# A decoder trunk in which the output projection becomes two Strassen products around the pointwise projection

## Chip, cores and metric

The kernel runs on one core of a Trainium2 chip. The metric is device microseconds (us) of one execution; a run's time is that of the whole program. TensorE is PE in the profile (PEld is its weight load), VectorE is DVE, ScalarE is ACT, GpSimd is POOL, and SyncE, which issues the kernel's DMAs, is SP.

## The reference

The kernel computes one layer for 1024 tokens and a model width of 1024:

```python
u = rms_norm(x, ln_g)
c_val, c_glu, c_gate, hq, hf, hi, hg = split(u @ w_in)       # seven parts of 1024 columns
y_conv = conformer(c_val, c_glu) @ w_pw2 + b_pw2             # pointwise projection
y_conv = y_conv * silu(c_gate)                               # the conv gate
y_hgrn = hgrn2(hq, hf, hi) * silu(hg)                        # eight heads of 128
h = x + concat([y_conv, y_hgrn]) @ w_out                     # w_out: 2048 x 1024
gate = sigmoid(rms_norm(h, pe_norm_g) @ w_pg)
h = h + gate * (p @ w_pp)
out = rms_norm(h, final_g)
```

All is float32. Every matrix product on PE is made of two float32r parts of each factor, a high part and the rest, as high x high + high x low + low x high: three matmuls for one.

## The kernel before

Tokens are cut into eight blocks of 128, and for moving operands into two halves of 512; channels into eight blocks of 128. A split of an operand (`split`) is a copy on ACT into the high part and a subtraction on DVE into the low part. `prep` loads a weight block into a tile `raw` of the pool `wp`, which has three buffers of it, and splits it.

**The z stage** takes u (in SBUF, split, channels on partitions) through w_in, one block of 128 columns at a time: `ztile` preps the block and `product` makes two PSUM banks with 48 matmuls. The loop over the eight heads and channel groups does the conv and the heads; it leaves the conv's result in DRAM (`yc_d`) and each head's in `yh_d` (the tile sgT, whose last step are two multiplications on DVE, L443, that read the banks ot of PE's transposes). Last come the eight conv gates (`conv_gate`, column blocks 16 to 23, tiles wz16 to wz23): ACT takes the SiLU into sgc, and SP writes it to `sg_d`.

**The pointwise projection** loads yc into the pool `yp`, split (tiles ych, ycl). For each of eight column blocks m it preps wpw, loads the gate (sgr), makes two banks, and DVE adds the bias and multiplies with the gate (L570). The result is split at once into mch, mcl and stays in SBUF.

**The output projection** then takes 16 row blocks of w_out (eight for the pointwise result, eight for the heads, whose tiles yhr are loaded and split here into mhh, mhl) for the first four token blocks, with eight banks open: one per token block and column half. `residual` adds each bank to the residual h, a tile of x loaded into SBUF well ahead (L580, L595). A second pass does the other four token blocks, by column halves, with w_out loaded and split again. `norm_T` transposes the residual, scales and splits it. The gate's projection and the final norm are the tail.

Each engine takes its instructions in an order fixed when the program is built. A scheduler sets it: it takes the code in the order in which it is written, except where a `high_priority` number moves a step, as it does for the loads and splits of ztile's weights (2000 ahead) and for the late steps of heads and convs. A pool's tile with a tag is a ring of `bufs` buffers: a load into it waits until the last reader of the tile before it is done, and whatever stands behind that load on SP waits too.

Of the kernel before, what the change touches and what calls it, by code (L numbers as in the profile page):

```python
# [28 lines left out]
LATER_STATS, LATER_CONV, LATER_HEAD = 50, 330, 240  # L29
# columns of the transposed parameter table  # L30
# [5 lines left out]
def trunk_kernel(ctx: ExitStack, tc: tile.TileContext, x, p, ln_g, w_in, conv_w, conv_b,  # L36
# [12 lines left out]
    wp = ctx.enter_context(tc.tile_pool(name="wp", bufs=3))  # L49
    up = ctx.enter_context(tc.tile_pool(name="up", bufs=32))  # L50
# [10 lines left out]
    yh_d = [dpl.tile([P, T], F32, name=f"yh_d{m}") for m in range(G)]  # L61

    # ---------------------------------------------------------------- constants
# [7 lines left out]
    # per-channel parameters, channels on partitions  # L71
# [4 lines left out]
    def load_params(work):  # L76
# [11 lines left out]
        # lower bound: first row of the softmax over the layers  # L88
# [27 lines left out]
    def prep(src, shape, name):  # L116
        """A weight block: loaded, and split exactly into two float32r parts."""
# [13 lines left out]
    # ---------------------------------------------------------------- z phase  # L131
    uh = [[None] * G, [None] * G]
    ul = [[None] * G, [None] * G]
    with tc.tile_pool(name="st", bufs=1) as st:
        # layer embedding, projected: kept in DRAM until the gate is known
# [30 lines left out]
        def norm_x(hf, xs):  # L166
            """Normalised input of four token blocks, channels on partitions, split."""
# [14 lines left out]
        # masks[l][s, col]: where the key s is one that the score column couples to, the columns  # L182
        # being those of the block of 32 that s lies in
# [3 lines left out]
        def block_mask(dst, first, step_n, step_j, l):  # L187
            """Sets dst[s, n, j, i] where s is in the l keys from first + n step_n + j step_j."""
# [10 lines left out]
        def own_block(name, mf):  # L199
            """The columns of each row's own block out of those of the four blocks of 32."""  # L200
# [335 lines left out]
    for m in range(G):  # L536
        conv_gate(m)
# [16 lines left out]
    def load_split(src, hi, lo, k, name):  # L554
        raw = wp.tile([P, T], F32, tag="raw", name=name)
        nc.sync.dma_start(raw, src)
        for hf in range(2):
            split(hi[hf][k], lo[hf][k], halves(raw)[hf])

    ych, ycl = half_tiles(yp, "y", "yc")  # L560
    for k in range(G):
        load_split(yc_d[k], ych, ycl, k, f"ycr{k}")
# [167 lines left out]
```

## Time and profile before

| | us |
|---|---|
| median of three runs | 1146.96 |
| lowest, highest | 1146.39, 1148.70 |
| span of the profiled execution | 1146.5 |
| PE busy in it | 1124.8 |
| DVE, ACT, POOL busy in it | 739.5, 443.0, 72.0 |

The profiled execution is one run of the program; its span is 0.46 us under the median of the timed runs, and all rows below are from it. The last conv gates (blocks 20 to 23) run from 737.2 to 781.7 us, the pointwise projection from 781.7 to 868.7, the first half of the output projection from 868.7 to 955.7, the second half with the transposes around it from 955.7 to about 1050, and the gate's projection to the end. The page cuts the span into 40 slices of 28.7 us; a digit is the busy share of an engine in tenths. An engine's idle time counts only where what it holds up is on the way to the end.

### The profile page before, as it was taken

Reading aid. Unit: us, or ns where it says so; the run is one execution under the profiler, and the core shown is the slowest. Engines: PE = TensorE matmul, PEld = TensorE weight load, DVE = VectorE, ACT = ScalarE, POOL = GpSimd, SP = SyncE. Lnnn points to the kernel's source line nnn. Section 1 sums busy time; section 2 is a strip of 40 time slices with the busy share of each in tenths; the row PEclk is TensorE's granted clock in tenths of the full one; section 3 lists DMA queues with packets and bytes.
Section 4 is the critical chain, followed back from the end, with each engine's and each line's share of the span. In section 5 each row is a group of like instructions: output and inputs, shape, how many; then the busy total and the mean of one; then the engine's idle time right before and its main releaser. Section 6 shows DMA issues by size and latency. Waiting matters only on the chain.

```text
span 1146.5 us, 17744 instructions
## 1 busy us (share of the span) xinstructions
PE 1124.8 (98%) x7408; PEld 945.6 (82%) x7408; DVE 739.5 (65%) x1145; ACT 443.0 (39%) x811; POOL 72.0 (6%) x107
## 2 busy tenths in 40 slices
PE   6999999999999999999999999999999999999997
PEld 4888978889888789788898788888888888887886
DVE  3659579998499996599993896242334325226444
ACT  4823244253354442344532632442123324126333
POOL 3100001001001010010010010000000001001000
PEclk9899999999999999999999999999999999999999
DMA  7611121211111112111111112277335632334221
GB/s 247 236 37 55 37 66 30 74 55 39 55 57 56 59 35 74 56 37 56 57 56 56 57 56 93 74 242 254 110 92 165 195 99 77 107 109 149 92 92 56
DMA packets 85715, 104.60 MB, mean 91 GB/s; under 512 B 3290, under 2 KB 65754, under 8 KB 85634
## 3 DMA queue, kind: packets, MB, share of 16 engines
q1 hardware_dynamic: 85634, 103.46, 28.1%
q8 instruction: 58, 0.95, 0.3%
q14 instruction: 23, 0.19, 0.1%
HBM read 82.48 MB, written 20.97 MB: 90 GB/s over the span
## 4 chain that ended last, share of the span: by engine, by line
PE 89%; DVE 6%; DMA 2%; ACT 1%; issue 1%; SPq 0%; POOL 0%; POOLq 0%; ACTq 0%
PE z L241 14%; PE z L242 14%; PE z L243 14%; DVE y L452 4%; PE v L264 3%; PE v L265 3%; PE v L263 3%; PE pg L683 3%; PE pg L684 3%; PE pg L682 3%; PE oA L591 3%; PE pw L243 3%; PE pw L241 3%; PE oA L589 3%; PE oA L588 3%; PE pw L242 3%
## 5 line engine op out<-in xcount | busy, mean ns | idle before, releaser
L452 DVE SCALAR_TENSOR_TENSOR y<-vpad,par,y 128x1024 f32<-128x1024 f32 x232 | 288.8, 1278 | 1.1
L682 PE MATMUL pg<-gh,hh 128*128 128x512 f32 (+1 forms) x136 | 51.4, 378 | 0.0
L683 PE MATMUL pg<-gl,hh 128*128 128x512 f32 (+1 forms) x136 | 51.4, 378 | 0.0
L684 PE MATMUL pg<-gh,hl 128*128 128x512 f32 (+1 forms) x136 | 51.3, 377 | 0.0
L519 DVE TENSOR_TENSOR vpad<-z,gl 128x512 f32<-128x512 f32 x16 | 11.0, 691 | 42.7 <-PE z L243 42.7
L263 PE MATMUL v<-wv_0h,uh 128*128 128x256 f32 x128 | 36.7, 287 | 0.0
L265 PE MATMUL v<-wv_0h,ul 128*128 128x256 f32 x128 | 36.5, 285 | 0.0
L264 PE MATMUL v<-wv_0l,uh 128*128 128x256 f32 x128 | 36.5, 285 | 0.0
L263 PE MATMUL v<-wv_1h,uh 128*128 128x256 f32 x128 | 36.2, 283 | 0.0
L264 PE MATMUL v<-wv_1l,uh 128*128 128x256 f32 x128 | 36.2, 283 | 0.0
L265 PE MATMUL v<-wv_1h,ul 128*128 128x256 f32 x128 | 36.2, 283 | 0.0
L266 ACT ACTIVATE vt<-v 128x256 f32<-128x256 f32 x32 | 12.2, 382 | 58.9 <-PE v L265 58.9
L688 DVE TENSOR_TENSOR gt<-gt,pet 128x512 f32<-128x512 f32 (+1 forms) x17 | 11.2, 661 | 36.1 <-ACT gt L687 36.1
L108 POOL TENSOR_SCALAR ro<-sso 128x8 f32<-128x8 f32 x8 | 8.4, 1054 | 389.9 <-ACT on L129 389.9
L475 DVE TENSOR_SCALAR y<-yt,mv,ry 128x128 f32<-128x128 f32 x64 | 23.5, 404 | 13.1 <-POOL ry L109 13.1
L570 DVE SCALAR_TENSOR_TENSOR sgr<-pw,par,sgr 128x512 f32<-128x512 f32 x16 | 12.0, 750 | 30.1 <-PE pw L243 30.1
L437 ACT ACTIVATE on<-o,ro 128x128 f32<-128x128 f32 x64 | 18.5, 386 | 29.0 <-POOL ro L109 29.0
L682 PEld LDWEIGHTS pg<-gh,hh 128*128 128x128 f32 x136 | 25.6, 188 | 4.7
L683 PEld LDWEIGHTS pg<-gl,hh 128*128 128x128 f32 x136 | 25.6, 188 | 4.7
L684 PEld LDWEIGHTS pg<-gh,hl 128*128 128x128 f32 x136 | 25.6, 188 | 4.5
L483 ACT ACTIVATE yc<-yn,par 128x512 f32<-128x512 f32 x16 | 12.5, 778 | 39.8 <-PE yn L482 39.8
L129 ACT ACTIVATE on<-o 128x128 f32<-128x128 f32 x64 | 16.9, 278 | 23.3 <-PE up L409 18.9
(802 smaller groups left out, 3463.6 us busy)
## 6 DMA issues: line engine op xcount, KB each, us to landing
wz<-in_w_in_dram SPq DMA_DIRECT2D x48, 512.0 KB
wo<-in_w_out_dram SPq DMA_DIRECT2D x32, 512.0 KB
xt<-in_x_dram SPq DMA_DIRECT2D x8, 512.0 KB
pe_d<-pes SPq DMA_DIRECT2D x8, 512.0 KB
wv<-in_w_in_dram SPq DMA_DIRECT2D x8, 512.0 KB
yc_d<-yc SPq DMA_DIRECT2D x8, 512.0 KB
yh_d<-sgT SPq DMA_DIRECT2D x8, 512.0 KB
sg_d<-sgc SPq DMA_DIRECT2D x8, 512.0 KB
```

Source lines behind the costliest of these rows:

```text
L241: mm(z, lhsT=wh[:, k, :], rhs=mh[hf][k], start=k == 0, stop=False)
L242: mm(z, lhsT=wh[:, k, :], rhs=ml[hf][k], start=False, stop=False)
L243: mm(z, lhsT=wl[:, k, :], rhs=mh[hf][k], start=False, stop=k == G - 1)
L263: mm(z, lhsT=uh[hf][k][:, c], rhs=wh, start=k == 0, stop=False)
L264: mm(z, lhsT=uh[hf][k][:, c], rhs=wl, start=False, stop=False)
L265: mm(z, lhsT=ul[hf][k][:, c], rhs=wh, start=False, stop=k == G - 1)
L452: nc.vector.scalar_tensor_tensor(y[j % 2], vp[:, j:j + T], pcol(g, j), y[j % 2], op0=ALU.mult, op1=ALU.add)
L588: mm(z, lhsT=mixh[hf][k][:, c], rhs=wh[j], start=first, stop=False)
L589: mm(z, lhsT=mixh[hf][k][:, c], rhs=wl[j], start=False, stop=False)
L682: mm(z, lhsT=hh[k][:, c], rhs=gh[j][k][:, o:o + w], start=k == 0, stop=False)
L683: mm(z, lhsT=hh[k][:, c], rhs=gl_[j][k][:, o:o + w], start=False, stop=False)
L684: mm(z, lhsT=hl[k][:, c], rhs=gh[j][k][:, o:o + w], start=False, stop=k == G - 1)
```

## The change

The output projection is taken apart by halves of w_out. The heads' half is multiplied first, behind the conv gates; then comes the pointwise projection; then the half of the pointwise result, called the mixture. Each half is a product of 1024 tokens x 1024 channels x 1024 columns, done for one pair of token blocks after the other as a Strassen product (in Winograd's form): a pair's tokens, the channels' halves and the columns' halves make a 2 x 2 scheme, which takes seven products of 128 tokens x 512 channels x 512 columns instead of eight.

- `combos` loads the eight row blocks of a half of w_out (two at a time, each into a `raw`) and makes from them the seven weight combinations a, t1, t2, d, t3, c, t4, each in high and low part, 56 tiles in the new pool `cb`. For the heads' half it stands in the code between the fourth and the fifth conv gate and takes its `raw` from `wp`, whose ring wz20 shares; for the mixture's half it stands behind the first column block of the pointwise projection.
- `tokens` loads a pair's two channel halves (tiles mx) from DRAM, makes four sums on DVE and splits seven factors. `project` makes the seven products in three banks (za, zd, zb) that are never cleared in between; `put` adds or subtracts a bank into the two residual tiles as soon as a term of the sum is in it.
- The heads' residual tiles hx are loaded from x, one buffer for each block of a pair, and written to `h_d` behind the pair. Behind the pointwise projection they are loaded back into eight tiles h.
- The pointwise result goes to DRAM (`mc_d`) and its loads are those of `tokens`. The weights wpw now come as two halves from the pool `rg`, in tiles `s` that the yc loads and the sums share (four buffers).
- The gate's weights and the transposed residual take over tiles of `cb`; `norm_T` for both halves stands behind all pairs.
- The scratch for dynamic DMAs is set to 2048 bytes.

```diff
@@ the output projection's weights, and where they stand @@
-    for m in range(G):
+    def combos(row0, pool, bufs):
+        hi = {n: [] for n in XN}
+        lo = {n: [] for n in XN}
+        def part(n, k, src, sign=1.0):
...
+            nc.scalar.activation(h, src, AF.Copy, scale=sign)
+            nc.vector.scalar_tensor_tensor(lo[n][k], src, sign, h.bitcast(F32),
+                                           op0=ALU.mult, op1=ALU.subtract)
+        for k in range(KH):
+            rows = []
+            for i in range(2):
+                r = pool.tile([P, D], F32, tag="raw", bufs=bufs, name=f"wo{row0}_{k}_{i}")
+                o = row0 + (i * KH + k) * P
+                nc.sync.dma_start(r, w_out[o:o + P, :])
+                rows += halves(r)
+            a, b, c, d = rows
+            for n, t in (("a", a), ("c", c), ("d", d)):
+                part(n, k, t)
+            nc.vector.tensor_tensor(a, a, b, op=ALU.subtract)
+            part("t1", k, a)
+            nc.vector.tensor_tensor(a, a, d, op=ALU.add)
+            part("t2", k, a, -1.0)
+            nc.vector.tensor_tensor(b, d, b, op=ALU.subtract)
+            part("t3", k, b)
+            nc.vector.tensor_tensor(c, a, c, op=ALU.subtract)
+            part("t4", k, c)
+        return hi, lo
+    for m in range(G // 2):
         conv_gate(m)
+    xh, xl = combos(D, wp, 3)
+    for m in range(G // 2, G):
+        conv_gate(m)
@@ a pair of token blocks @@
+    def tokens(src, tb):
+        r0, r1 = (raw(src[i * H:(i + 1) * H, tb * P:(tb + 2) * P]
+                      .rearrange("(k p) t -> p k t", p=P), f"mx{src.name}{tb}_{i}")
+                  for i in range(2))
...
+    def project(src, tb, hA, hB):
+        f1, f5, f6, f3, f7, f2, f4 = tokens(src, tb)
+        za, zd, zb = (bank("z", f"o{n}{src.name}{tb}") for n in "adb")
...
+        mul(za, f1, "a", True, False)
+        put(hA, 0, za, ALU.add)
+        mul(zd, f5, "t1", True, False)
+        put(hB, 1, zd, ALU.subtract)
+        mul(za, f6, "t2", False, False)
+        put(hA, 1, za, ALU.add)
+        mul(zd, f3, "d", False, True)
+        put(hA, 1, zd, ALU.add)
+        mul(za, f7, "t3", False, False)
+        put(hB, 1, za, ALU.subtract)
+        mul(zb, f2, "c", True, True)
+        put(hA, 0, zb, ALU.add)
+        mul(za, f4, "t4", False, True)
+        put(hB, 0, za, ALU.subtract)
@@ the heads' half, ahead of the pointwise projection @@
+    with tc.tile_pool(name="hx", bufs=1, reuse_waits="tile") as hx:
+        for tb in range(0, G, 2):
+            hAB = []
+            for i in range(2):
+                t = hx.tile([P, D], F32, tag=f"h{i}", name=f"hx{tb + i}")
+                nc.sync.dma_start(t, x[(tb + i) * P:(tb + i + 1) * P, :])
+                hAB.append(t)
+            project(yh_d, tb, *hAB)
+            for i in range(2):
+                nc.sync.dma_start(h_d[tb + i], hAB[i])
@@ the pointwise projection @@
+            if m == 1:
+                xh, xl = combos(0, rg, 2)
...
+            nc.sync.dma_start(mc_d[m * P:(m + 1) * P, :], sg)
@@ the mixture's half @@
+    hs = [hp.tile([P, D], F32, name=f"h{tb}") for tb in range(G)]
+    for tb in range(G):
+        nc.sync.dma_start(hs[tb], h_d[tb])
...
-    hhA, hlA = norm_T(0)
...
+    for tb in range(0, G, 2):
+        project(mc_d, tb, hs[tb], hs[tb + 1])
```

**DVE between gate blocks 19 and 20.** Before, DVE does the last head's state (S) and its two last steps sgT (banks ot), with the low parts of wz22 and wz23 around them; wz20l and wz21l are further up:

```order
L414 SCALAR_TENSOR_TENSOR S_6583<-S_6583,F_128_6580,up_0_6596 128x128 x3
L414 SCALAR_TENSOR_TENSOR S_6583<-S_6583,F_128_6580,up_1_6605 128x128 x3
L114 TENSOR_TENSOR wz22l<-wz_7024,wz22h 128x1024
L443 SCALAR_TENSOR_TENSOR sgT_6019<-ot_0_6646,par,sgT_6019 128x512
L114 TENSOR_TENSOR wz23l<-wz_7084,wz23h 128x1024
L443 SCALAR_TENSOR_TENSOR sgT_6019<-ot_1_6656,par,sgT_6019 128x512
L114 TENSOR_TENSOR ycl_0_7151<-ycr_7182,ych_0_7150 128x512
```

Now these two last steps are followed by the 44 operations of the first combinations (al, cl, dl, t1l and so on; the rows L576 to L582 are their sums), and wz20l stands behind the 42nd of them:

```order
L448 SCALAR_TENSOR_TENSOR sgT_6021<-ot_0_6648,par,sgT_6021 128x512
L448 SCALAR_TENSOR_TENSOR sgT_6021<-ot_1_6658,par,sgT_6021 128x512
L563 SCALAR_TENSOR_TENSOR al_0_6914<-wo_0_0_6909,ah_0_6913 128x512
L563 SCALAR_TENSOR_TENSOR cl_0_6918<-wo_0_1_6911,ch_0_6917 128x512
L563 SCALAR_TENSOR_TENSOR dl_0_6922<-wo_0_1_6911,dh_0_6921 128x512
L576 TENSOR_TENSOR wo_0_0_6909<-wo_0_0_6909 128x512
...
L563 SCALAR_TENSOR_TENSOR t3l_3_7045<-wo_3_0_7017,t3h_3_7044 128x512
L119 TENSOR_TENSOR wz20l<-wz_7054,wz20h 128x1024
L582 TENSOR_TENSOR wo_3_1_7019<-wo_3_0_7017,wo_3_1_7019 128x512
L563 SCALAR_TENSOR_TENSOR t4l_3_7050<-wo_3_1_7019,t4h_3_7049 128x512
L119 TENSOR_TENSOR wz21l<-wz_7114,wz21h 128x1024
L119 TENSOR_TENSOR wz22l<-wz_7174,wz22h 128x1024
```

The low parts of all four last gate blocks moved behind the combinations, and nothing else stands between the steps sgT and them.

**SP from the last gates to the next stage.** Before, the loads of the pointwise operands (ycr) are mixed with the writes of the gates (sg_d) and the first residual loads:

```order
L556 DMA ycr0_7182<-yc_d0_81 128x1024
L491 DMA sg_d3_76<-sgc3_6843 128x1024
L556 DMA ycr1_7188<-yc_d1_82 128x1024
L491 DMA sg_d4_77<-sgc4_6903 128x1024
L445 DMA yh_d7_96<-sgT7_6019 128x1024
L556 DMA ycr2_7194<-yc_d2_83 128x1024
L580 DMA h0_7806<-in_x_dram 128x1024
L580 DMA h1_7807<-in_x_dram 128x1024
L556 DMA ycr3_7200<-yc_d3_84 128x1024
```

Now the first loads of the heads' pair (mxyh_d) stand behind the last gate's write (sg_d7) and both residual loads hx0, hx1:

```order
L124 DMA wz23_7234<-in_w_in_dram 128x8x128
L496 DMA sg_d4_77<-sgc4_7053 128x1024
L496 DMA sg_d5_78<-sgc5_7113 128x1024
L496 DMA sg_d6_79<-sgc6_7173 128x1024
L667 DMA hx0_7304<-in_x_dram 128x1024
L496 DMA sg_d7_80<-sgc7_7233 128x1024
L667 DMA hx1_7306<-in_x_dram 128x1024
L597 DMA mxyh_d_890_0_7308<-yh_d_89 128x4x256
L597 DMA mxyh_d_890_1_7310<-yh_d_89 128x4x256
```

The operands of the stage behind the gates moved from ahead of the gates' last writes to behind them.

**SP at the end of the pointwise projection.** Before, the last weights and gates of the pointwise projection (wpw, sgr) are followed by the first row blocks of w_out and by the first head's tile:

```order
L119 DMA wpw6_7646<-in_w_pw2_dram 128x8x128
L567 DMA sgr6_7652<-sg_d6_79 128x1024
L119 DMA wpw7_7710<-in_w_pw2_dram 128x8x128
L567 DMA sgr7_7716<-sg_d7_80 128x1024
L119 DMA wo0_7830<-in_w_out_dram 128x1024
L119 DMA wo1_7836<-in_w_out_dram 128x1024
L119 DMA wo2_7842<-in_w_out_dram 128x1024
L556 DMA yhr0_7848<-yh_d0_89 128x1024
L119 DMA wo3_7878<-in_w_out_dram 128x1024
L556 DMA yhr1_7884<-yh_d1_90 128x1024
```

Now the writes of the pointwise result (mc_d) stand there, then eight residual loads, then the second half of the mixture's first pair (mxmc_d_900_1):

```order
L695 DMA sgr7_8589<-sg_d7_80 128x1024
L705 DMA mc_d_90<-sgr6_8522 128x1024
L705 DMA mc_d_90<-sgr7_8589 128x1024
L711 DMA h0_8649<-h_d0_91 128x1024
L711 DMA h1_8650<-h_d1_92 128x1024
L711 DMA h2_8651<-h_d2_93 128x1024
L711 DMA h3_8652<-h_d3_94 128x1024
L711 DMA h4_8653<-h_d4_95 128x1024
L711 DMA h5_8654<-h_d5_96 128x1024
L711 DMA h6_8655<-h_d6_97 128x1024
L711 DMA h7_8656<-h_d7_98 128x1024
L597 DMA mxmc_d_900_1_8667<-mc_d_90 128x4x256
```

A load that waits for nothing of the stage before (wo0) gave its place to writes of that stage's last results, and to a load that reads them.

## Rows read from the trace of the kernel before

**Rows 1.** the page: the span, the busy shares, PE in 40 slices.

```profile
span 1146.5 us, 17744 instructions
...
PE 1124.8 (98%) x7408; PEld 945.6 (82%) x7408; DVE 739.5 (65%) x1145; ACT 443.0 (39%) x811; POOL 72.0 (6%) x107
...
PE   6999999999999999999999999999999999999997
```

**Rows 2.** windows by stage: us, busy time of each engine, PEclk, DMA share, GB/s.

```profile
781.70:868.70 87.00, 87.00 (x385) 72.09 (x384) 32.14 (x41) 18.94 (x26) 0.00 (x0) 1.00 0.41 132
868.70:955.70 87.00, 87.00 (x385) 72.06 (x385) 32.31 (x37) 24.91 (x31) 0.00 (x0) 1.00 0.48 151
```

**Rows 3.** what PE waited for: us in total, times, longest us.

```profile
PE pt L85 <- DMA prow<-in_lb_logits_dram: 4.6, 1, 4.6
...
PE ht L626 <- DVE h L595: 0.9, 1, 0.9
```

**Rows 4.** timeline of PE, second matmuls of the pointwise projection: start, us.

```profile
781.71 0.39 PE L241 MATMUL pw<-ych,wpw0h 128*128 128x512 f32 x1
781.93 0.39 PE L242 MATMUL pw<-ycl,wpw0h 128*128 128x512 f32 x1
```

**Rows 5.** timeline of PE: eight transposes; end of block 19, start of 20.

```profile
688.63 1.03 PE L462 MATMUL yt<-ident,y 128*128 128x128 f32 x8
...
736.97 0.39 PE L243 MATMUL z<-uh,wz19l 128*128 128x512 f32 x1
737.19 0.39 PE L241 MATMUL z<-uh,wz20h 128*128 128x512 f32 x1
```

**Rows 6.** timeline of DVE: low part of wz20, the last steps sgT, low parts.

```profile
703.96 1.23 DVE L114 TENSOR_TENSOR wz20l<-wz,wz20h 128x1024 fp32r<-128x1024 f32 x1 [2.02 <-ACT wz20h L113]
...
747.61 0.75 DVE L443 SCALAR_TENSOR_TENSOR sgT<-ot,par,sgT 128x512 f32<-128x512 f32 x1 [8.12 <-PE ot L441]
...
755.90 3.70 DVE L114 TENSOR_TENSOR ycl<-ycr,ych 128x512 fp32r<-128x512 f32 x6 [4.39 <-ACT ych L113]
```

**Rows 7.** ACT's groups from 700 us on: count, busy us, mean ns, idle before.

```profile
L113 ACT ACTIVATE ych<-ycr 128x512 fp32r<-128x512 f32 x16 | 9.0, 624 | 5.6 <-DMA ycr<-yc_d 5.6
L490 ACT ACTIVATE sgc<-z 128x512 f32<-128x512 f32 x13 | 7.7, 593 | 14.1 <-PE z L243 12.0 <-DMA sg_d<-sgc 2.1
```

**Rows 8.** timeline at three loads: issue on SP, first use on ACT.

```profile
757.22 1.53 SPq L556 DMA_DIRECT2D ycr<-yc_d  x2
...
763.20 2.33 ACT L113 ACTIVATE ych<-ycr 128x512 fp32r<-128x512 f32 x4 [2.46 <-DMA ycr<-yc_d]
...
827.60 0.38 SPq L119 DMA_DIRECT2D wpw<-in_w_pw_dram  x1
...
831.89 1.06 ACT L113 ACTIVATE wpw6h<-wpw 128x1024 fp32r<-128x1024 f32 x1 [5.05 <-DMA wpw<-in_w_pw_dram]
...
871.11 0.33 SPq L556 DMA_DIRECT2D yhr<-yh_d  x1
...
874.89 0.63 ACT L113 ACTIVATE mhh<-yhr 128x512 fp32r<-128x512 f32 x1 [4.52 <-DMA yhr<-yh_d]
```

**Rows 9.** windows of 10 us while the pointwise operands load: DMA share, GB/s last.

```profile
755.00:765.00 10.00, 10.00 (x46) 8.29 (x45) 4.83 (x8) 5.85 (x12) 0.00 (x0) 1.00 0.94 326
765.00:775.00 10.00, 10.00 (x46) 8.29 (x45) 5.25 (x9) 5.28 (x11) 0.00 (x0) 1.00 0.87 274
```

**Rows 10.** timeline of PE at its wait in the first stage.

```profile
22.99 0.39 PE L230 MATMUL pe<-wpp1h,pTl 128*128 128x512 f32 x1
28.03 1.04 PE L85 MATMUL pt<-ident,prow 40*128 40x40 f32 x8 [4.65 <-DMA prow<-in_lb_logits_dram]
```

**Rows 11.** windows of 1 us behind that wait: PEclk is the third last.

```profile
28.00:29.00 1.00, 0.97 (x8) 0.92 (x8) 0.00 (x0) 0.00 (x0) 0.00 (x0) 0.50 1.03 422
33.00:34.00 1.00, 1.00 (x6) 1.00 (x5) 0.75 (x1) 1.00 (x4) 0.00 (x0) 0.50 1.05 418
...
35.00:36.00 1.00, 1.00 (x8) 0.82 (x7) 0.00 (x0) 1.00 (x4) 0.67 (x2) 1.00 1.08 336
```

More of the change, by code (lines that the diff above doesn't have):

```diff
@@ L60, in trunk_kernel @@
     yc_d = [dpl.tile([P, T], F32, name=f"yc_d{m}") for m in range(G)]
-    yh_d = [dpl.tile([P, T], F32, name=f"yh_d{m}") for m in range(G)]
+    yh_d = dpl.tile([D, T], F32, name="yh_d")
+    mc_d = dpl.tile([D, T], F32, name="mc_d")
+    h_d = [dpl.tile([P, D], F32, name=f"h_d{tb}") for tb in range(G)]
     ident = cst.tile([P, P], F32, name="ident")
@@ new lines, in project, with mul, put @@
+    def project(src, tb, hA, hB):
+        f1, f5, f6, f3, f7, f2, f4 = tokens(src, tb)
+        za, zd, zb = (bank("z", f"o{n}{src.name}{tb}") for n in "adb")
+        def mul(z, f, n, first, last):
+            wh, wl = f
+            for k in range(KH):
+                mm(z, lhsT=wh[:, k, :], rhs=xh[n][k], start=first and k == 0, stop=False,
+                   skip_group_check=True)
+                mm(z, lhsT=wh[:, k, :], rhs=xl[n][k], start=False, stop=False,
+                   skip_group_check=True)
+                mm(z, lhsT=wl[:, k, :], rhs=xh[n][k], start=False, stop=last and k == KH - 1,
+                   skip_group_check=True)
+        def put(h, j, z, op):
+            h = halves(h)[j]
+            with tc.high_priority(SOON):
+                nc.vector.tensor_tensor(h, h, z, op=op)
+        mul(za, f1, "a", True, False)
[12 more added lines that the diff above has]
+        put(hB, 0, za, ALU.subtract)
@@ L548, in half_tiles @@
         for hf in range(2):
             for k in range(G):
-                hi[hf][k] = pool.tile([P, H], F32R, tag=tag, name=f"{name}h{hf}_{k}")
-                lo[hf][k] = pool.tile([P, H], F32R, tag=tag, name=f"{name}l{hf}_{k}")
-        return hi, lo
[L554 to L560, printed above, removed]
@@ L561, in trunk_kernel @@
-    for k in range(G):
-        load_split(yc_d[k], ych, ycl, k, f"ycr{k}")
-    mch, mcl = half_tiles(up, "u", "mc")
-    for m in range(G):
-        wh, wl = prep(colblock(w_pw2, m * P), [P, G, P], f"wpw{m}")
-        sg = wp.tile([P, T], F32, tag="raw", name=f"sgr{m}")
-        nc.sync.dma_start(sg, sg_d[m])
-        for hf, z in enumerate(product(wh, wl, ych, ycl, "z", f"pw{m}")):
-            s = halves(sg)[hf]
-            nc.vector.scalar_tensor_tensor(s, z, pcol(m, R_BPW), s, op0=ALU.add, op1=ALU.mult)
-            split(mch[hf][m], mcl[hf][m], s)
@@ L578, in trunk_kernel @@
+    yctx.close()
+    hp = ctx.enter_context(tc.tile_pool(name="hp", bufs=1, reuse_waits="tile"))
     hs = [hp.tile([P, D], F32, name=f"h{tb}") for tb in range(G)]
     for tb in range(G):
[L580 to L591 removed]
@@ L613, in trunk_kernel, with norm_T @@
-    for j in range(2):
-        for b in range(4):
-            residual(0, b, j, zs[b, j])
+        nc.sync.dma_start(hs[tb], h_d[tb])
     rs = [None] * G
-    def norm_T(hf):
+    def norm_T(hf, tags):
         hh = [None] * G
@@ L699, in trunk_kernel @@
         for j in range(2):
-            nc.sync.dma_start(out[tb * P:(tb + 1) * P, j * H:(j + 1) * H], halves(ot)[j])
+            nc.sync.dma_start(out[tb * P:(tb + 1) * P, j * H:(j + 1) * H], ot[j])
 _INS = ['x', 'p', 'ln_g', 'w_in', 'conv_w', 'conv_b', 'cnorm_g', 'cnorm_b', 'w_pw2', 'b_pw2',
```

151 lines of the change are left out of this document (86 added, 65 removed).

## The prediction

> **What bounds the kernel now.** I read the busy shares, then the stage windows, then what PE waited for, and last the queues at the places that the change rewrites. PE is busy 1124.8 of 1146.5 us and its slices stay at 9 from the second to the last but one [rows 1]. The stages to be rewritten are full: 87.00 of 87.00 us in the pointwise projection and again in the first output half, while DVE does 32 us there [rows 2]. Behind the first 50 us PE's longest wait is 0.9 us, for the last residual add [rows 3]. So nothing stands in front of PE now, and two things count: how many matmuls there are, and whether something new stands in front of it. A matmul's price is its spacing: 384 of them fill 87.0 us [rows 2], 0.2266 us each, as the starts at 781.71 and 781.93 show [rows 4]. The 0.39 us in those rows is a pipelined duration; what it has over the spacing, rounded to 0.2, I take below for the hand-over from PE to whoever reads its last result.
>
> The Trainium skill ("TensorE: Matmul & The Clock Gate", Back-to-back issue gap) puts a sustained stream of 512-column matmuls at about 131 ns apiece. By it the 96 matmuls below would be worth 12.6 us; the rows show 226.6 ns here, and the sum goes by them.
>
> **What the change takes away.** The output projection was 2 token halves x 16 row blocks x 4 token blocks x 2 column halves x 3 = 768 matmuls. It becomes 2 x 4 pairs of token blocks x 7 products x 4 row blocks x 3 = 672. 96 fewer x 0.2266 = **21.8 us**, all of it on PE, and all on the path as long as PE stays fed. A product (12 matmuls) is then 2.72 us, a pair (84) 19.0 us. In a pair DVE gets 4 sums, 7 low parts and 7 adds into the residual, 18 operations of about 0.62 us (six in 3.70 [rows 6]): 11 us under 19. The average is covered; the hand-overs between stages are what must be priced. Before, each next stage's operands were loaded and split under the last one's matmuls.
>
> **Hand-over A, gate block 19 to 20.** The order shows on DVE: the last two steps of the last head (sgT), 42 operations of the first weight combinations, and only then wz20l. ACT has the same order, and SP issues wz20's load behind all eight w_out loads, because both share `raw`. Before, wz20 was ready long before and sgT7 came 10 us later. sgT7 needs ot7, which PE now does behind block 19. So PE finishes block 19 at 737.2 [rows 5] and eight transposes (1.03 [rows 5]) at 738.2, then has nothing: 2 x 0.75 (sgT [rows 6]) + 42 x 0.617 + 1.23 (wz20l) = 28.6 us until the third matmul of block 20. On top come loads: `raw` has three buffers, so in pairs 1, 2 and 3 the second row block is loaded into a buffer freed two to four DVE operations before it is needed. A 512 KB load takes 3.8 us from issue to use (871.11 to 874.89), 4.3 for the weights in short rows (827.60 to 831.89), up to 6.0 in a crowd (757.22 to 763.20) [rows 8]; 3.8 less 1.2 to 2.5 us of work is 1.3 to 2.6, some 5.5 us for the three. **34 us**; 28.6 if no load is late, 43 if each takes 6.0 and so do its writes.
>
> **Hand-over B, gate block 23 to the heads' products.** SP has sg_d7's write, which waits for ACT's last SiLU (0.60 [rows 7]), ahead of hx1 and of both loads of the heads' mixture; hx0 waits for PE's last matmuls, in whose tiles it lies. From PE's end: 0.2 + 0.6, and three issues of 0.4 (0.33 to 0.38 [rows 8]), the last one the mixture's own, 2.0 us. The load lies behind sg_d7 and hx1; at 326 GB/s (DMA 0.94 busy [rows 9]) 512 KB is 1.6 us, so 3.8 + 2.4 to land, and 0.8 for ACT's split (0.62 [rows 7] and as much as a hand-over): **9 us**; 6.6 without the queue, 12 with 6.0 us landings.
>
> **Residual through DRAM, within the heads' products.** hx has one buffer per block: write h_d, then load the next x into it. The write of hx0 starts 1.8 us before the pair ends and lands 2.0 us after it; the load lands at 6.0, DVE, blocked on that add, does it by 6.8, and the third product, which reuses the bank, could have begun at 5.4. About 1.5 us for each of three pairs, **5 us** with rounding; 2 if half as late, 17 with landings of 6.0.
>
> **Hand-over C, heads to pointwise.** On DVE, behind the last residual add, stand eight operations of the yc parts and of the next combinations up to ycl1_4, whose `s` buffer the first load of wpw0 takes. 0.9 (hand-over and add) + 8 x 0.62 = 5.9, issue 0.4, landing 3.8, split 0.8: **11 us**; 9 to 13.5.
>
> **Hand-over D, pointwise to the mixture's products.** The first product needs only channels 0 to 511, long written: 2.7 us of cover. The second needs mc_d7, which PE has just made. From PE's end: DVE's 0.95 (0.2 and an operation of 0.75), the write, and then SP issues eight residual loads (h0 to h7) ahead of the mixture's second half. Write, eight loads and the half are ten transfers of 1.6 = 16, the fixed part of a landing is 3.8 - 1.6 = 2.2, then add and split 1.6, with 0.95 + 0.4 ahead: 21.2 - 2.7 = **18.5 us**. If the loads did not hold it up: 0.95 + 0.35 + 3.8 (write) + 0.4 + 3.8 + 1.6 - 2.7 = 8.2. At the 274 GB/s of the next window [rows 9]: 21.5.
>
> **The clock.** After PE's 4.65 us of idling from 23 us on [rows 10] the granted clock was 0.50 (1.2 GHz), and stood there while PE worked from 28.0 to about 34.5 us [rows 11]: 6.5 us at half speed, 3.25 us lost. A to D are all longer than that idle stretch: 4 x 3.25 = **13 us**; 6.5 if half of it falls into waits that are there anyway.
>
> The Trainium skill (the same page, Loop structure matters more than you think) speaks against such a loop: a wait for DMA ahead of the matmuls makes PE run cold. This trace agrees at its one such place. By the rule the sum has the 13 us; with the row read as an accident of the start it hasn't, and the kernel stands at 1204.
>
> **What is hidden.** The second weight combinations (44 DVE operations, 27 us) lie under 87 us of pointwise matmuls, where DVE now does 32 us [rows 2]; without that cover they would cost what A costs. Within the mixture's products the residual lies in SBUF and each add has the 2.7 us of a product in another bank. Behind them the last gate weights' splits stand ahead of the transposes' on ACT: **1 us** (0 to 2). The smaller DMA scratch moves no instruction, and no row prices it: 0.
>
> **Sum.** 34 + 9 + 5 + 11 + 18.5 + 13 + 1 = 91.5, less 21.8 = 69.7. On the profiled span of 1146.5 that is 1216.2; the median of the timed runs lies 0.5 above the span, so **1217 us**. All low ends: 60.9 - 21.8 = 39, 1186. All high ends: 122 - 21.8 = 100, 1247.
>
> **Rivals.**
> - Residual loads do not hold up the mixture's half, D costs 8.2: 1207. For it: they wait for nothing but pw7_0, and the write stands ahead of them. Against it: at 0.94 busy the DMA engines have no room, and the order puts them first. 0.2.
> - The residual chain and all landings go by 6.0 us, as in the crowded stretch: +12 and some 10 more, about 1235. For it: 3 MB in 19 us. 0.15.
> - The clock does not fall: 1204. Only one place speaks for the fall, but nothing against it. 0.05.
> - A is covered, DVE working through the combinations during block 19: 1217 - 37 = 1180. Against it: sgT7 is ahead of them in the same queue. 0.03.
> - Faster: every hand-over is covered, PE takes the 21.8 us, 1125. It is one mechanism: queues that run far enough ahead of PE. Its place is the head of DVE's and SP's queues at z20, at the mixture and at mc_d, and it decides from the point where all gaps together fall under 21.8 us. A alone is above that, unless PE is no longer waiting for wz20. 0.02.
>
> **How the numbers follow.** The forecast has 0.55. From 1186, all low ends, to 1240 the range holds the forecast with most of its bounds, the first, the third and most of the second rival; 1180, 1125 and what is above 1240 stay out, under 0.2. A measurement of this kernel can tell 0.2% (2.3 us) from no change. Faster 0.02, within it 0.01, slower 0.97.
>
> **What the profile will show.** Right: PE idle by over 28 us between the blocks 19 and 20, with ACT wz20h as its releaser; gaps of about 9, 11 and 18 us at the first matmul of the heads' products, of pw0 and of the mixture's second product; the clock at 0.5 behind each; 0.227 us between matmuls elsewhere. Wrong in A: PE goes from block 19 to 20 without a wait. Wrong in D: the mixture's half lands before h7. Wrong in the gain: a pair takes more than 21 us in the mixture's products, where no gap is expected. What would overturn all: DVE's combinations starting before sgT7.

## The result, and the profile after

| | before | after |
|---|---|---|
| median, us | 1146.96 | 1214.62 |
| lowest, highest | 1146.39, 1148.70 | 1212.95, 1217.44 |
| span of the profiled execution | 1146.5 | 1215.6 |

The changed kernel takes 1.059 times as long (95% interval 1.0574 to 1.0607). Its profiled execution is the slowest of its four runs, so the spans differ by 69.1 us and the medians by 67.7; the stages below are compared by spans. The page of after, the lines that answer to [rows 1] and the granted clock in the same 40 slices (30.4 us each):

```profile
PE 1124.5 (92%) x7312; PEld 935.9 (77%) x7312; DVE 817.2 (67%) x1305; ACT 461.5 (38%) x867; POOL 73.2 (6%) x107
...
PE   7999999999999999999999992688996994999997
...
PEclk9999999999999999999999996798997997999999
```

96 matmuls are gone (7408 to 7312), but PE is busy as long as before (1124.5 against 1124.8 us): most of what the change took away came back as slower matmuls (11.5 us by the clock and 5.8 by their spacing, both below). Its idle time grew from 21.7 to 91.1 us, and that is the loss. The slices that were all 9 now have a 2, a 4 and two of 6, and the clock has a dent at each. What PE waited for says which (line, releaser: us in total, times, longest):

```profile
PE z L246 <- ACT wz20h L118: 32.1, 1, 32.1
PE odmc_d L633 <- ACT fmc_d_1h L118: 15.3, 1, 15.3
PE pw L700 <- ACT wpw_0h L118: 11.6, 1, 11.6
PE oayh_d L633 <- ACT fyh_d_0h L118: 8.3, 1, 8.3
...
PE oayh_d L633 <- DVE hx L643: 2.0, 3, 1.3
PE pg L778 <- ACT hh L727: 1.6, 1, 1.6
PE obyh_d L633 <- ACT fyh_d_5h L118: 1.5, 3, 0.5
```

Before, the longest wait behind the first 50 us was 0.9 [rows 3]. The four large ones are A, D, C and B of the prediction, oayh_d behind hx (2.0) is the residual's chain through the pairs, and pg the norm. obyh_d (1.5) is none of the prediction's terms: from the second pair on, the first matmuls of the sixth product stand ahead of the third product, and its factor is split into a ring of four buffers, into the one of the second product, which PE has only just ended (ACT waits 2.1 us for it at 852).

**A.** The timeline of PE and DVE around block 20 (start, us, engine, line, operation; in brackets the idle time ahead and its releaser):

```profile
736.97 1.03 PE L446 MATMUL ot<-ident,on 128*128 128x128 f32 x8
770.12 0.79 PE L246 MATMUL z<-uh,wz20h 128*128 128x512 f32 x1 [32.12 <-ACT wz20h L118]
...
771.13 0.63 PE L246 MATMUL z<-uh,wz20h 128*128 128x512 f32 x1
771.56 0.63 PE L248 MATMUL z<-uh,wz20l 128*128 128x512 f32 x1
```

```profile
737.60 1.41 DVE L448 SCALAR_TENSOR_TENSOR sgT<-ot,par,sgT 128x512 f32<-128x512 f32 x2 [8.78 <-PE ot L446]
...
770.10 1.23 DVE L119 TENSOR_TENSOR wz20l<-wz,wz20h 128x1024 fp32r<-128x1024 f32 x1 [0.51 <-ACT wz20h L118]
```

PE ends its transposes at 738.0. DVE does sgT from 737.6 on and then goes through the combinations one behind the other, every 0.60 us, with three waits for loads (2.55, 0.90 and 0.96), and only then makes wz20l. It had idled 8.8 us ahead of sgT, with the first row blocks of w_out issued since 694: their splits stood behind the last head's steps on DVE and behind block 19's SiLU on ACT. But the row of wz20l has 0.51 us of idling for ACT's wz20h in it, so DVE's order is not what ended last. The chain that did, followed back from block 20 (start, us, what):

```profile
764.16 4.82 DMA wz<-in_w_in_dram
...
769.01 1.07 ACT wz20h L118
```

SP could issue wz20's load only at 764.16, when the 35th of the 44 operations (t4l of the third pair of row blocks, done at 764.1) had freed a `raw` buffer. The load took 4.8 us, the split 1.1. DVE's own route, all 42 operations and then wz20l, would have ended half a microsecond sooner. The first matmuls of block 20 then stand 0.427 us apart, not 0.227.

**B and D.** SP's issues and the instruction that waits for them:

```profile
816.97 0.32 SPq L496 DMA_DIRECT2D sg_d<-sgc  x1
817.33 0.43 SPq L667 DMA_DIRECT2D hx<-in_x_dram  x1
817.86 1.46 SPq L597 DMA_DIRECT2D mxyh_d<-yh_d  x2
...
823.93 0.63 ACT L118 ACTIVATE fyh_d_0h<-mxyh_d 128x512 fp32r<-128x512 f32 x1 [6.99 <-DMA mxyh_d<-yh_d]
```

```profile
1014.06 5.03 SPq L711 DMA_DIRECT2D h<-h_d  x8
1019.13 0.44 SPq L597 DMA_DIRECT2D mxmc_d<-mc_d  x1
...
1029.51 0.69 DVE L615 TENSOR_TENSOR smc_d<-mxmc_d,mxmc_d 128x512 f32<-128x512 f32 x1 [10.03 <-DMA mxmc_d<-mc_d]
```

At B the load goes out behind sg_d and hx and is used 6.1 us later. At D eight residual loads go first, as forecast; the half behind them is used 10.4 us after its issue. Windows of D and of the clock (us, busy time of PE, PEld, DVE, ACT, POOL, then PEclk, DMA share, GB/s):

```profile
772.00:775.00 3.00, 3.00 (x9) 2.32 (x8) 0.69 (x1) 0.59 (x1) 0.00 (x0) 0.50 0.83 241
...
1020.00:1023.00 3.00, 0.00 (x0) 0.00 (x0) 0.00 (x0) 0.00 (x0) 0.00 (x0) 0.66 1.03 419
...
1029.00:1032.00 3.00, 1.00 (x2) 0.78 (x3) 2.41 (x4) 1.26 (x2) 0.00 (x0) 0.50 0.23 89
1113.00:1116.00 3.00, 3.00 (x14) 2.65 (x13) 2.85 (x5) 1.84 (x4) 0.00 (x0) 0.52 0.00 0
```

From 742 on the clock stood at 0.50 (1.2 GHz) through A, and until 775, when PE had been at work again for 5 us; from 775 to 778 it was 0.96. It was 0.50 behind each of the four gaps (behind B in the window from 826 to 829, behind C from 925 to 928), and 0.52 in a place that the prediction did not name, the start of the gate's projection.

**Between the gaps.** Matmuls of a Strassen product:

```profile
842.02 0.40 PE L635 MATMUL obyh_d<-cl,fyh_d_5h 128*128 128x512 f32 x1
842.26 0.39 PE L637 MATMUL obyh_d<-ch,fyh_d_5l 128*128 128x512 f32 x1
```

They start 0.2333 us apart (the mean over the heads' products), not 0.2266. A product takes 2.80 us, a pair 19.6. This was not expected.

By stages, from the start times of PE: block 20 starts 32.9 us later (A); from there to the heads' products 10.0 us more (B and A's clock); the pointwise stage 3.05 more (C's clock); the two output halves with the rest, 300.9 against 277.8, 23.15 more (C, D, the pairs, less the gain). Together 69.1.

### The profile page after: what moved, and what is told of

It reads as the page before. It is cut to its first block, busy times and chain, and to the rows that moved or that the text cites. A ratio compares the mean times of both kernels' runs of the same rounds, so it can differ in the third digit from the quotient of the medians.

```text
span 1215.6 us, 17917 instructions
## 1 busy us (share of the span) xinstructions
PE 1124.5 (92%) x7312; PEld 935.9 (77%) x7312; DVE 817.2 (67%) x1305; ACT 461.5 (38%) x867; POOL 73.2 (6%) x107
## 4 chain that ended last, share of the span: by engine, by line
PE 77%; DVE 10%; DMA 10%; ACT 2%; issue 1%; SPq 1%; POOL 0%; POOLq 0%; DVEq 0%; ACTq 0%
PE z L246 13%; PE z L247 13%; PE z L248 13%; DVE y L457 4%; PE v L270 3%; PE v L269 3%; PE v L268 3%; PE pw L700 3%; PE pw L701 2%; PE pw L702 2%; PE pg L780 2%; PE pg L779 2%; PE pg L778 2%; DMA mxyh_d<-yh_d 1%; PE sc L300 1%; DMA mxmc_d<-mc_d 1%
## 5 line engine op out<-in xcount | busy, mean ns | idle before, releaser
L246 PE MATMUL z<-uh,wz20h 128*128 128x512 f32 x16 | 7.6, 474 | 32.1 <-ACT wz20h L118 32.1
L700 PE MATMUL pw<-ych,wpw_0h 128*128 128x512 f32 x64 | 26.0, 407 | 11.6 <-ACT wpw_0h L118 11.6
```

The lines of the kernel that those rows point to most:

```text
L246: mm(z, lhsT=wh[:, k, :], rhs=mh[hf][k], start=k == 0, stop=False)
L700: mm(z, lhsT=wh, rhs=ych[hf][k], start=k == 0, stop=False)
```

## Experiments

The theory: the time is lost where a fixed queue makes an operand of the next stage wait behind work of another, at A to D, and each gap costs the clock on top. The rivals are named with each run. All are edits of the changed kernel, but for one of the kernel before. Times are medians, ratios are to the kernel before, timed beside each run.

**A: the combinations behind the gates.**

```diff
-    for m in range(G // 2):
+    for m in range(G):
         conv_gate(m)
     xh, xl = combos(D, wp, 3)
-    for m in range(G // 2, G):
-        conv_gate(m)
```

> Only the place of the first weight combinations is changed: behind all eight conv gates instead of between the fourth and the fifth. Theory (DVE's queue is the wait A): PE goes from gate block 19 to 20 without the 32.1 us wait and without the half-speed stretch behind it (12 matmuls at 0.427 instead of 0.227 us, 2.4 us); the 44 DVE operations (27 us and some 5 us of loads) lie under the 44 us of blocks 20 to 23, so the gap ahead of the heads' products stays near 8.3 us. Time 1214.6 - 34.5 = 1180. Rival 1 (the gap only moves): the heads' products wait for the last combinations, gap B grows to 20 us or more, time 1192 or above. Rival 2 (block 20 waits for something else, its load or the raw ring): the 32 us stay, time about 1214.

1179.43 us, ratio 1.0283 (1.0266 to 1.0300). The wait at block 20 is gone, and 35.2 us with it; the gaps behind it stand as they were:

```profile
PE odmc_d L631 <- ACT fmc_d_1h L118: 15.3, 1, 15.3
PE pw L698 <- ACT wpw_0h L118: 11.8, 1, 11.8
PE oayh_d L631 <- ACT fyh_d_0h L118: 8.9, 1, 8.9
```

The same 44 operations on DVE cost next to nothing here, where they stand behind the last head's steps and beside blocks 20 to 23 (B went from 8.3 to 8.9). A was their place, not their amount. The edit moves wz20 ahead of them in the order of DVE, ACT and SP at once; which of the three held it is told by the chain of after alone.

**The clock: PE kept busy in gap A.** 132 matmuls whose result nobody reads are put into the gap.

```diff
     xh, xl = combos(D, wp, 3)
+    warm = bank("t", "warm")
+    with tc.high_priority(300):
+        for i in range(132):
+            mm(warm, lhsT=xl["a"][0][:, :P], rhs=uh[0][1], start=True, stop=True)
     for m in range(G // 2, G):
```

> 132 matmuls whose result nobody reads are added on PE behind the last head's transposes, so that PE works instead of waiting ahead of gate block 20; they end before the weights come. Theory (idling lowers the clock): block 20 starts at the same time as before, about 770 us, but at 1.00 granted clock, and its first 12 matmuls take 0.227 instead of 0.427 us: 2.4 us sooner at block 21, the whole 1212. Rival (the half speed belongs to the place, for instance to a load or a split beside it): the clock is 0.50 at block 20 all the same, time 1214.6 or later.

1209.39 us (one run), 5.2 less than the median of after; by spans it is 8.0 less (1207.6 against 1215.6). The window in which block 20 starts:

```profile
768.00:771.00 3.00, 3.00 (x14) 2.22 (x13) 2.06 (x3) 0.64 (x1) 0.00 (x0) 1.00 0.29 85
```

Block 20 starts at 768.32 with the clock at 1.00 and takes 51.49 us to the heads' products instead of 54.49. Of these 3.0 us, 0.7 are a shorter wait B (7.6, not 8.3). So idling lowers the clock, and that costs 2.3 us here, near the 2.4 of 12 matmuls at 0.427 instead of 0.227, the gap itself left as it is. Block 20 also starts 1.8 us earlier; it does so in runs that leave A alone too (768.34 with the pad below, 768.52 with the early weights), so that part need not be an effect of the edit.

**D: which transfer stands first.** The loads h2 to h7 go behind the mixture's second half.

```diff
-    for tb in range(G):
-        nc.sync.dma_start(hs[tb], h_d[tb])
+    load_h((0, 1))
...
         f1, f5, f6, f3, f7, f2, f4 = tokens(src, tb)
+        loads()
...
-        project(mc_d, tb, hs[tb], hs[tb + 1])
+        project(mc_d, tb, hs[tb], hs[tb + 1], lambda: load_h(range(2, G) if tb == 0 else ()))
```

> Of the eight residual loads at the end of the pointwise projection only the first two stay ahead of the mixture's second half; the other six follow behind it. Theory (the loads hold up the half): the 15.3 us gap ahead of the second product falls to what the sum gave without the loads, 8.2, or 7 to 9; time 1214.6 - 7 = 1207.5. Rival (the gap is the write of the last pointwise block and its reading back, not the loads): the gap stays within 1.5 us of 15.3, time 1213 to 1215. Rival 2 (the six loads now meet the products' adds of the second pair): a new wait at the second pair, time 1210 or more.

1204.68 us, ratio 1.0505 (1.0489 to 1.0521):

```profile
PE odmc_d L634 <- ACT fmc_d_1h L118: 7.4, 1, 7.4
```

15.3 became 7.4: the six residual loads did hold up the half. What is left is the round through DRAM with h0 and h1 still ahead of the half, for which the prediction, without any load, had 8.2.

**D: the round through DRAM.** The last pointwise block is written in two token halves as each is made, so that the first pair's tokens wait for the first of them only.

```diff
                 nc.vector.scalar_tensor_tensor(s, z, pcol(m, R_BPW), s, op0=ALU.add, op1=ALU.mult)
-            nc.sync.dma_start(mc_d[m * P:(m + 1) * P, :], sg)
+                if m == G - 1:
+                    nc.sync.dma_start(mc_d[m * P:(m + 1) * P, hf * H:(hf + 1) * H], s)
+            if m < G - 1:
+                nc.sync.dma_start(mc_d[m * P:(m + 1) * P, :], sg)
```

> The last pointwise block is written to memory in two halves of 512 tokens, the first as soon as it is made, 5.4 us before the second; the first pair of the mixture needs the first only, and its second half of channels is now loaded ahead of the second write and of the eight residual loads. Theory (D is the way of the last block through memory, behind the residual loads): of the 15.3 us gap 0 to 3 us stay at the second product; the first add into the residual now ends last, h0 landing some 4 to 6 us behind PE's end, and the third product may wait up to 3 us for it; time 1214.6 - 13 = 1201.5, with the clock's 2 us 1199.5. Rival (the eight loads and the pair's loads share the DMA engines, so that the sum of bytes decides): the gap stays above 8 us, time 1207 or more.

1196.62 us, ratio 1.0428 (1.0412 to 1.0444), 18.0 less than after. The second product waits for nothing; of D there remains one wait of 0.5 us, at obmc_d. The write of the first half and the load of the mixture's half now run under the last 24 pointwise matmuls (5.4 us) and the first product (2.8), and the load goes ahead of h0 to h7 too. Of the 18.0, 14.8 are the gap and 1.7 the clock behind it. The clock also stayed at 1.00 at the start of the gate's projection, where after lost some 1.8.

**C: the first pointwise weights earlier.** They are loaded and split between the eighth and the ninth operand of yc, not behind all sixteen. `pw_weights` holds the lines that stood in the loop over m.

```diff
         for hf in range(2):
+            if hf:
+                fs0 = pw_weights(0)
             for k in range(G):
...
-                fs = []
...
+                fs = pw_weights(m) if m else fs0
```

> The first pointwise weights (wpw0) are loaded and split between the first eight and the last eight of the yc loads, instead of behind all sixteen. Theory (the load of wpw0 waits in the ring s and on SP behind the yc loads and DVE's low parts): the 11.6 us gap ahead of the pointwise projection falls to 3 to 5 us, what is left being the last of the first eight yc tiles; time 1214.6 - 7.5 = 1207. Rival (the yc tiles themselves are late, the weights only come last): the gap stays above 9 us and names ych or ycl, time 1212 to 1215.

1200.29 us, ratio 1.0460 (1.0445 to 1.0475), lower than expected:

```profile
PE pw L706 <- ACT ych L118: 0.7, 1, 0.7
PE pw L707 <- DVE ycl L119: 0.2, 1, 0.2
```

I had left 3 to 5 us for the operands loaded behind the weights; it is 0.9, and the first product ran at full clock. 14.3 us is the gap (11.6 less 0.9) and some 3 of clock.

**The spacing: 32 bytes.** In the built program the tiles of cb start 32 bytes past a multiple of 64. A tile of 32 bytes per partition ahead of that pool moves them onto one.

```diff
+    pad = ctx.enter_context(tc.tile_pool(name="pad", bufs=1, side="right"))
+    pad.tile([P, 8], F32, name="pad32")
     cb = ctx.enter_context(tc.tile_pool(name="cb", bufs=1, side="right", reuse_waits="tile"))
```

> 32 bytes are put at the end of the memory, so that the pool of weight combinations, whose tiles begin 32 bytes behind a multiple of 64, begins at a multiple of 64; nothing else changes. Theory (the start address of the moving operand sets the spacing): matmuls of the Strassen products go from 0.2333 to 0.2266 us, 672 x 0.0067 = 4.5 us, and those of the gate's projection that read this pool as moving operand (half of 384) another 1.3: 1208.8 us. Rival (the spacing comes from the products' use of banks that are never cleared, or from their weight tiles): 0.2333 stays, time 1214.6.

1210.54 us, ratio 1.0550 (1.0532 to 1.0567), 4.1 less than after, where 5.8 were expected (the wait C was 1.3 us longer in it). First matmuls of two products that follow each other, and the one behind it:

```profile
1045.52 0.39 PE L635 MATMUL oamc_d<-ah,fmc_d_0h 128*128 128x512 f32 x1
1045.74 0.39 PE L637 MATMUL oamc_d<-al,fmc_d_0h 128*128 128x512 f32 x1
...
1048.23 0.39 PE L635 MATMUL odmc_d<-t1h,fmc_d_1h 128*128 128x512 f32 x1
```

2.71 us a product (2.72 by most of them) and 0.2266 a matmul. Nothing else about them was changed, so the start address of the operand makes the difference; the gate's projection, half of it slow in after, runs at 0.227 throughout.

**The same 32 bytes in the kernel before.** The pad stands there ahead of the pool yp, whose tiles are the moving operand of the pointwise projection and, later, the weights of the heads' half of the output projection.

```diff
+    pad = ctx.enter_context(tc.tile_pool(name="pad", bufs=1))
+    pad.tile([P, 8], F32, name="pad32")
     yp = ctx.enter_context(tc.tile_pool(name="yp", bufs=32, reuse_waits="tile"))
```

> The kernel before, with 32 bytes put ahead of the pool of the pointwise operands and the residual, so that its tiles begin 32 bytes behind a multiple of 64; nothing else changes. Theory (the start address of the moving operand sets the spacing, that of the weights does not): the 384 matmuls of the pointwise projection go from 0.2266 to 0.2333 us and those of the gate's projection too, 768 x 0.0067 = 5.1 us: 1152; the output projection, where this pool gives weights only, keeps 0.2266. Rival 1 (it belongs to the form of the Strassen products): no change, 1146.9. Rival 2 (weights count too): the second half of the first output half also goes to 0.2333, 1153.5 or more.

1153.76 us, ratio 1.0062 (1.0048 to 1.0077): the kernel before is 7 us slower for 32 bytes that nobody uses.

```profile
790.34 0.40 PE L242 MATMUL pw<-ycl,wpw0h 128*128 128x512 f32 x1
790.57 0.39 PE L243 MATMUL pw<-ych,wpw0l 128*128 128x512 f32 x1
```

The pointwise matmuls went from 0.2267 to 0.2333. So did those of the gate's projection, whose moving operand is in yp too. In the first output half, those whose weights are mhh (in yp) went to 0.2333 and those whose weights are mch stayed at 0.2269. So the address counts for the stationary operand too, which I had given to the rival. In all, some 1150 matmuls at 0.0067 us are 7.7.

**Both operands shifted.** The trace of after has a case that neither run was made for. In its gate's projection the stationary operand (hh, hl) always lies in cb, 32 bytes past a multiple of 64. In the built program the weights of the first column half (24 matmuls of each token block) lie in hp, on a multiple; those of the second half, the next 24, lie in cb as well. Nine intervals of a first half, and nine of the second half behind it, past its first six matmuls:

```profile
1186.40 0.40 PE L778 MATMUL pg<-gh,hh 128*128 128x512 f32 x1
...
1188.50 0.40 PE L778 MATMUL pg<-gh,hh 128*128 128x512 f32 x1
...
1193.37 0.39 PE L778 MATMUL pg<-gh,hh 128*128 128x512 f32 x1
...
1195.41 0.39 PE L778 MATMUL pg<-gh,hh 128*128 128x512 f32 x1
```

2.10 us against 2.04: 0.2333 a matmul where the two operands start differently, 0.2267 where both start 32 bytes past. Of the other token blocks, those that run at full clock and without transposes between them show the same. So what goes with the loss is that the two starts differ, not that one of them is off the multiple.

**All repairs together.** A, C, both edits of D and the pad as above; SiLU writes, the first pair's x and h0, h1 issued from ACT's queue; the heads' residual of pairs 2 and 4 in free tiles of yp (so that a pair's write and the next load need no common buffer).

> All edits in one: combinations behind the conv gates, their pool at a multiple of 64 bytes, wpw0 early, the last pointwise block in halves, six of the residual loads behind the mixture's first loads; the gates' writes and the four residual loads ahead of the first pairs are issued by ACT instead of SP, so that the heads' first loads no longer stand behind them; the residual tiles of the heads' second and fourth pair have buffers of their own. Theory (the waits are what eats a real gain of 21.8 us): left are some 2 us of B, 4 of C, 1 to 3 of D, 1.5 of the norm and 2 to 5 of clock; time 1125 + 13 to 16 and 3 for the rest, 1138 to 1145, below the 1146.7 of the kernel before. Rival (the Strassen form costs more elsewhere, in DVE work or transfers, than its 96 matmuls): PE waits in new places inside the pairs, time 1150 or more.

1147.61 us, ratio 1.0003 (0.9995 to 1.0012): a miss. What was left:

```profile
PE oayh_d L634 <- ACT fyh_d_0h L118: 5.1, 1, 5.1
...
PE oamc_d L634 <- DVE h L644: 5.0, 1, 5.0
...
PE pg L802 <- ACT hh L751: 2.9, 1, 2.9
```

The second one I had made myself. SP sends h2 to h7 from 958.03 to 961.25, and ACT, busy with the splits ahead of it, issues h0 at 959.40, when they are under way; it lands 7.2 us later.

A second variant took the residual back to one buffer for each block of a pair and put two row blocks of the first combinations into other tiles than `raw`.

> As e7, with two differences taken from its trace: the heads' residual tiles have one buffer again, so that the residual tiles of the mixture lie where the first half of the yc tiles lay, free 5.4 us before the pointwise projection ends; and two of the eight row blocks of w_out are loaded into buffers of the gates' weight parts instead of the ring of three, so that DVE does not wait for loads among the first combinations. Theory (what is left in e7 are waits for buffers): the 5.0 us wait for h0 goes, that ahead of the heads' products falls from 5.1 to 1 to 3, the one behind it (1.2) goes, and with them some 4 us of half speed: 1147.6 - 12 = 1135 to 1139. Rival (the transfers share the same bandwidth and the waits only change their names): 1144 or more.

1153.87 us, ratio 1.0070 (1.0056 to 1.0085), another miss:

```profile
PE oayh_d L635 <- ACT fyh_d_0h L118: 10.3, 1, 10.3
...
PE oayh_d L635 <- DVE hx L645: 3.1, 3, 2.2
```

With one buffer the chain through the pairs is back (3.1), and the wait for h0 stayed (4.7). The runs with one buffer show 0.4 to 3.1 us for that chain, the two with a second one at most 0.4, so the second buffer is likely what takes it away; no run changes it alone. The heads' loads went out at 783.31 only, as DVE ended the last combination (783.27), with both hx and the last sg_d already under way: their tiles lie where `raw` did. The row blocks to move were the last two. That is the third variant, with the buffers of the first and all h loads on SP again, behind the mixture's half:

```diff
-                r = pool.tile([P, D], F32, tag="raw", bufs=bufs, name=f"wo{row0}_{k}_{i}")
+                tag = ("hi", "lo")[i] if row0 and k == 3 else "raw"
+                r = pool.tile([P, D], F32, tag=tag, bufs=bufs, name=f"wo{row0}_{k}_{i}")
```

> As e7, with two differences: the eight residual loads of the mixture stay on SP, all behind the second half of the last pointwise block (as in e6, where the mixture's first pair had no wait for them), and the last row block of the first combinations lies in buffers of the gates' weight parts, so that the first loads of the heads' pair no longer wait for the last combinations (in e7 the second of them did, until 786.6, and in e8 both, until 783.3). Theory (what is left in e7 are waits for buffers and queues): the 5.0 us wait for h0 goes, that ahead of the heads' products falls from 5.1 to 1 to 3, the two behind it (1.2 and 0.5) go, with them some 4 us of half speed; 1147.6 - 12 = 1133 to 1139, below the 1146.7 of the kernel before. Rival (the combinations' own length, 44 operations from 750.8 on, sets the start of the heads' products): the wait there stays above 4 us, time 1140 to 1143.

1138.84 us against 1147.53, ratio 0.9931 (0.9918 to 0.9945): faster than the kernel before by 8.7 us.

```profile
PE oayh_d L634 <- ACT fyh_d_0h L118: 4.5, 1, 4.5
...
PE pg L798 <- ACT hh L747: 2.2, 1, 2.2
...
786.22 0.80 PE L634 MATMUL oayh_d<-ah,fyh_d_0h 128*128 128x512 f32 x1 [4.46 <-ACT fyh_d_0h L118]
...
791.51 0.63 PE L634 MATMUL odyh_d<-t1h,fyh_d_1h 128*128 128x512 f32 x1
```

The time lies in the range expected, the wait at the heads' first operand does not: it is 4.5, not 1 to 3, which was the sign of the rival. ACT's queue shows why:

```profile
783.54 0.63 ACT L564 ACTIVATE t4h<-wo 128x512 fp32r<-128x512 f32 x1 [1.77 <-DVE wo L585]
...
785.54 0.63 ACT L118 ACTIVATE fyh_d_0h<-mxyh_d 128x512 fp32r<-128x512 f32 x1 [0.89 <-DMA mxyh_d<-yh_d]
```

PE ends block 23 at 781.8. The last split of the combinations waits for DVE until 783.5, and the last SiLU, two issues and the first factor's split stand behind it. So the combinations, which cost next to nothing in the first experiment, set this start once the loads no longer do.

A pair takes 19.04 us. Of the 21.8 us that the 96 matmuls are worth, 4.5 go at the heads' first operand, 2.6 at its clock (the first product takes 5.29 us, not 2.72), 2.2 at the norm and 1.2 in short waits: 10.5. That leaves 11.3; measured are 8.7 by medians and 9.8 by spans. The rest is not traced.

## Why the prediction was right, and where it was not

1217 was predicted, 1214.62 came. By its steps:

| step | predicted, us | measured in after |
|---|---|---|
| A | 34 | 32.1 |
| B | 9 | 8.3 |
| residual chain of the heads' pairs | 5 | 2.0, and 1.5 at obyh_d |
| C | 11 | 11.6 |
| D | 18.5 | 15.3 |
| clock | 13 | 11.5 |
| norm | 1 | 1.6 |
| 96 matmuls fewer | -21.8 | -16.0 |
| sum | 69.7 | 67.9 of 69.1 |

**A, B, C** hold in place, releaser and size. A was reckoned as 28.6 us on DVE, with wz20l as its last step, and 5.5 of late loads. The first experiment shows that the combinations ahead of block 20 are the cause. The path was another at its end: 26.2 us until the 35th operation freed the buffer (3.5 of them waits for loads), then wz20's load (4.8) and its split (1.1). The prediction named that load's place on SP but put no price on it. That the two routes end within half a microsecond of each other is luck. C's cause is shown by the fifth experiment; from PE's end to the issue of its load it is 5.9 us, as in the sum. B's was not taken away alone: in the last variant, with other edits around it, the wait is 4.5 and is set by the combinations.

**D** has the right mechanism: the third experiment takes away the share of six of the loads (7.9 us) and leaves the round through DRAM (7.4), and the rival in which the loads hold nothing up falls. The term was 3 us too large, by the rate as far as the windows tell: the sum used 326 GB/s [rows 9], and the windows of D show up to 419. Two of the rows behind the clock already showed such a rate [rows 11]; 326 was from a stretch with other work beside it.

**The clock** fell behind all four gaps, as said; the keep-busy run shows at A that idling causes it. The Trainium skill ("TensorE: Matmul & The Clock Gate", Loop structure matters more than you think) has it that waiting for DMA ahead of matmuls makes PE run cold; this trace and that run agree (0.50 behind waits of 8.3 to 32.1 us, 1.00 at block 20 where PE was kept busy). The term was sized by the one row of before, 3.25 us a gap. The first products show 2.5, 2.5, 3.0 and 1.7 at A, B, C, D, 9.7 together, and some 1.8 came at the start of the gate's projection, where no loss was reckoned.

**The gain is the step that failed.** The prediction took the spacing of before for the new tiles, and bounded it by nothing. 672 matmuls at 0.0067 us more are 4.5 us. Of the gate's projection 192 lose another 1.3: those whose weights lie in hp while their other operand had moved into cb, not those with both in cb, as the expectation of the pad had it. The two alignment runs show the cause. "A pair takes more than 21 us" was set too coarse to catch a pair of 19.6.

**The sum** is better than its terms: the waits and the clock are 83.9 instead of 91.5, and the gain is 5.8 smaller. The errors cancel, which is luck, and 1.2 us is in no term. The verdict was not in doubt with A alone above the whole gain (32.1 against 21.8); nor would it have been without A, since no repair by itself comes near the kernel before. The second rival's figures, 1217 with 12 and 10 more, add up to 1239 and not to 1235; nothing hangs on it. The rival "every hand-over covered, 1125" was right in its mechanism, as the last variant shows, though it needed all the edits together and reached 1138.84.

## What to carry to other kernels

Price a change that saves matmuls by the queues in front of each next stage: what stands at the head of DVE's, ACT's and SP's order when PE needs the next operand, and which buffer its load waits for. Work that is covered on the average (44 operations beside four gate blocks) cost 35 us ahead of an operand that PE waits for, and next to nothing behind it. Look also at what the operand's own load waits for: a ring shared with that work holds it just as long. Write a result that the next stage reads through DRAM in the pieces that its first reader needs, and keep the loads that are needed late behind those needed now, on the same queue. When a pool is added, look whether the two operands of a matmul still start alike.

## What the runs showed of the hardware

**Operand addresses.** A float32r matmul of 128 x 128 by 128 x 512 took 0.2266 us from start to start with both operands on a multiple of 64 bytes, and 0.2333 with one of them 32 bytes past it (3.0% more). It was so for the moving operand (Strassen products, pointwise projection) and for the stationary one (0.2267 to 0.2333 in the first output half). With both 32 bytes past it, in half of the gate's projection of after, it was 0.2267 again. Only these two offsets were tried.

**The clock behind short waits.** After a wait of 1.6 us at the start of the gate's projection of after, the granted clock was 0.52 in the window from 1113 to 1116; in the last variant the same place had a wait of 2.2 us and the clock stayed at 1.00:

```profile
1035.00:1038.00 3.00, 2.27 (x14) 1.80 (x15) 2.87 (x5) 3.00 (x7) 0.00 (x0) 1.00 0.01 3
```

The length of the wait alone does not tell these apart: in that place the clock also fell behind 1.7 (early weights) and 1.9 us (pad), and stayed at 1.00 behind 1.8 (last block in halves) and 2.9 us (all repairs). What does was not tried, and stays open.

**Transfers.** At D the DMA engines moved 419 GB/s from 1020 to 1023 us, with the residual loads, the mixture's half and one load for the tail under way.
